# Keys, memories and values of a decoder step's cross-attention loaded through GpSimd's queue, one step earlier and by a clock of emitted work

## The chip, the cores and the metric

The kernel runs on one core of a Trainium2 chip. The metric is the device time of one execution in microseconds (us), as the median of several runs. TensorE is called PE in the profile (PEld is its weight load), VectorE DVE, ScalarE ACT, GpSimd POOL, SyncE SP.

## What is computed

One step of a one-layer decoder on 256 prompt tokens and 64 sample tokens (8 requests of 8 tokens) that share all weights, in float32. A mixer (retention heads beside a gated short convolution), a cross-attention over 256 memory tokens, and a SwiGLU feed-forward; each adds to the residual. The prompt's memory keys and values are products of this step; those of the eight sample requests come from a cache in HBM.

```python
def memory_kv(mem, ln_mem_g, w_mk, w_mv):
    B, N, _ = mem.shape
    hm = rmsnorm(mem, ln_mem_g)
    mk = (hm @ w_mk).reshape(B, N, XA_HEADS, XA_DIM)
    mv = (hm @ w_mv).reshape(B, N, XA_HEADS, XA_DIM)
    return mk, mv

def memory_xattn_sublayer(x, ln_g, w_xq, w_xo, mk, mv):
    B, T, _ = x.shape
    h = rmsnorm(x, ln_g)
    q = (h @ w_xq).reshape(B, T, XA_HEADS, XA_DIM).astype(jnp.float32)
    s = jnp.einsum('bthd,bnhd->bhtn', q, mk.astype(jnp.float32)) * (XA_DIM ** -0.5)
    p = jax.nn.softmax(s, axis=-1)
    o = jnp.einsum('bhtn,bnhd->bthd', p, mv.astype(jnp.float32)).reshape(B, T, D_MODEL)
    return x + o.astype(x.dtype) @ w_xo
```

Here XA_HEADS is 4, XA_DIM 512, D_MODEL 2048. The sample requests' keys and values are 16 MB each.

## The kernel before

Every product with a weight runs as three matmuls per tile (`mm3`, L163 to L165): activations and weights are split into a high and a low float32r part. `Weights` streams the weights: SP loads a chunk of 512 KB (`w_raw`, four buffers, three loaded ahead), ACT casts a piece of 128x512 to `w_hi` (L121), DVE subtracts for `w_lo` (L122). Five buffers of each part let ACT and DVE run three pieces ahead of PE. One piece is two k-rows of a product with 320 columns (twelve matmuls), or one k-row of `w_mk` or `w_mv` with 512 columns (six).

PE, ACT and DVE execute in the order in which the program text emits (`manual_schedule`), POOL and SP in theirs. Work beside the products is written as generators in a queue, `background`; after every piece `tick(rate)` lets the first generator go on by one `yield`.

The stages in order, in us of the profiled execution: retention and convolution products to 454.6; the product with `w_mix_out` (called the mixer's output product) to 567.3, in eight groups `g` of eight pieces, each followed by `residual` (L704); the product with `w_xq` in eight groups to about 700; per head of four, the products with `w_mk` and `w_mv`, to 941; the product with `w_xo` to 1066; the feed-forward to the end.

`residual` does for each of two rows `m`: DVE adds the product to `x_res` (L707), `split_gain` makes `a_hi` (ACT, L244) and `a_lo` (DVE, L245), and `add_square` (L292) lets ACT write the square to `sq_t` (L297), of which there is one buffer, and POOL add it to `sq_sum` (L298).

The cross-attention's side work:

- `fetch_memory` and `fetch_keys` load the prompt's memories and the samples' keys, 512 KB a tile, as four DMAs of 32 partitions each on SP's queue, into three buffers `keys`.
- `memory_tiles` turns a memory tile on DVE (L783), multiplies by the gain (L788), squares on ACT (L790) and splits into `mem_hi`, `mem_lo`, which lie in the mixer's buffers `b_hi`, `b_lo`. It begins with the product with `w_xq`.
- `sample_head(h)`, for each head and each half `p` of the requests: DVE turns four key tiles (L851) into four buffers `kt`, PE makes the scores (L860). Then `load_values` (L813) loads four tiles of 512 KB into the same four buffers on SP's queue, the exponents follow, and PE multiplies with the values (L887). The second half's values are loaded when the first's product has been emitted, with `PACE` (5) yields between.
- `prompt_scores`, `prompt_values` do the prompt's part of a head, from the fresh `mk` and `mv`. `kv` (one buffer) is written by ACT (L1006) and sent out on POOL's queue (L1007).

Of the kernel before, what the change touches and what calls it, by code (L numbers as in the profile page):

```python
# [11 lines left out]
F32 = mybir.dt.float32  # L12
# [24 lines left out]
RATE_RET, RATE_XQ, RATE_KV = 0.9, 1.0, 1.0  # L37
PACE = 5
# [97 lines left out]
def step_kernel(ctx, tc, a, o):  # L136
# [80 lines left out]
    def drain():  # L217
        while background:
            credit[0] = 1.0
            tick(0.0)  # L220

# [197 lines left out]
    def continue_product(acc, xh, xl, nk, rate, k_from, k_to, k_first=0):  # L419
        done = k_from  # L420
        while done < k_to:
# [7 lines left out]
            tick(rate)  # L429

# [8 lines left out]
    with tc.tile_pool(name="ret", bufs=2, reuse_waits="tile") as ret:  # L439
# [162 lines left out]
        for pair in range(4):  # L602
# [27 lines left out]
            if pair == 0:  # L630
# [5 lines left out]
                hold_b.tile([P, 120], F32, name="fill_b")  # L636
# [84 lines left out]
    for g in range(8):  # L721
        residual(g, product(b_hi, b_lo, KT, 0.25), LN_XA, a_hi, a_lo)
    background.append(norm_table(XD ** -0.5))


    with tc.tile_pool(name="att", bufs=1, reuse_waits="tile") as att:
        q_p = att.tile([P, KT, TP], F32, name="q_p")
# [5 lines left out]
        xq_done = []  # L733
# [6 lines left out]
        def kv_tile():  # L740
            return att.tile([P, 1024], F32, tag="kt", name=uid("kt"), bufs=4)

        def misc_tile():
            return att.tile([P, 512], F32, tag="misc", name=uid("misc"), bufs=2)

# [19 lines left out]

        mem_order = deque(range(4))

        def fetch_memory():


            i = mem_order.popleft()
            t = att.tile([P, 8, P], F32, tag="keys", name=uid("mem"), bufs=3)
            for d in range(4):
                DMA.dma_start(out=t[32 * d:32 * d + 32].rearrange("p (n m) d -> p n (m d)", n=2),
                              in_=a["mem_prompt"][0, 64 * i:64 * i + 64, XD * d:XD * d + XD]
                              .rearrange("(n q) d -> q n d", q=32))
            keys.append(t)

        def memory_tiles():
            for i in range(4):  # L780
                t = keys.popleft()
                kt = kv_tile().rearrange("p (n k q) -> p n k q", k=KT, q=32)
                V.transpose(out=kt, in_=t.rearrange("p (n m) d -> p n (m d)", n=2)  # L783
                            .rearrange("p n (c k) -> p n k c", k=KT))
                flat = t.rearrange("p (n m) d -> p n (m d)", n=2)
                for n in range(2):
                    if n:
                        V.tensor_tensor(out=kt, in0=kt, in1=g_mem.unsqueeze(1).unsqueeze(3)  # L788
                                        .to_broadcast([P, 2, KT, 32]), op=ALU.mult)
                    S.activation(out=misc_tile(), in_=flat[:, n, :], func=AF.Square,  # L790
                                 accum_out=ssq_mem[:, i // 2, 2 * (i % 2) + n:2 * (i % 2) + n + 1])
                    yield
                (fetch_keys if i else fetch_memory)()
                for n in range(2):
                    hi, lo = (m[:, :, 64 * i + 32 * n:64 * i + 32 * n + 32]
                              for m in (mem_hi, mem_lo))
                    split(hi, lo, kt[:, n])
                    yield
# [8 lines left out]
            yield  # L807
# [37 lines left out]
        def sample_head(h):  # L845
            ss = mix_tile()
            for p in range(2):
                kts = []
                for j in range(4):
                    kt = kv_tile().rearrange("p (n d c) -> p n d c", d=4, c=32)  # L850
                    V.transpose(out=kt, in_=keys.popleft().rearrange("p n (d c) -> p n d c", c=32))  # L851
                    fetch_keys()
                    kts.append(kt)
                    yield
                for _ in range(2):
                    yield
                for d in range(4):
                    for j in range(4):

                        PE.matmul(ss[32 * j:32 * j + 32, NM * p:NM * p + NM]  # L860
                                  .rearrange("q (n c) -> q n c", c=32),
                                  q_s[:, 4 * h + d, 16 * j:16 * j + 32], kts[j][:, :, d, :],
                                  start=(d == 0), stop=(d == 3), tile_position=(0, 32 * j),
                                  skip_group_check=True)
# [251 lines left out]
```

## Time and profile before

| what | value |
|---|---|
| median of 3 runs | 2017.84 us (2017.77 to 2021.89) |
| the profiled execution, its time | 2018.07 us |
| its span, first to last instruction | 2016.3 us |
| busy PE / DVE / ACT / POOL | 98% / 53% / 42% / 6% |
| granted clock of PE, mean | 0.997 |
| moved by SP's queue / POOL's queue | 329.72 MB / 9.05 MB |

Busy time of PE is the union of its matmuls, whose ends are modelled; a PE that waits in the midst of a group of small matmuls can show as busy. A timeline row gives the start, the length, the engine, the line, the operation and, in brackets, idle time of the engine ahead of it and what ended that. The granted clock 1.00 is 2.4 GHz, 0.50 is 1.2 GHz.

### The profile page before, as it was taken

How to read it: one execution, taken by the hardware profiler on the slowest of the kernel's cores; microseconds unless marked ns; L12 is line 12 of the kernel's file. 1: busy time of each engine (PE TensorE's matmuls, PEld its weight loads, DVE VectorE, ACT ScalarE, POOL GpSimd, SP SyncE). 2: the span in 40 equal slices, each digit the busy share in tenths (PEclk: the TensorE clock that was granted, in tenths of full speed). 3: DMA queues.
4: the chain of work that ended last, by engine and by line, in shares of the span. 5: the costliest groups of instructions: out<-in, count | busy, mean ns of one | idle time of the engine just before them, and what ended most of it. 6: DMA issues, size and time to landing. Idle time of an engine off the chain costs nothing.

```text
span 2016.3 us, 34017 instructions
## 1 busy us (share of the span) xinstructions
PE 1985.9 (98%) x13310; PEld 1907.1 (95%) x13310; DVE 1076.1 (53%) x1931; ACT 840.9 (42%) x1648; POOL 123.5 (6%) x230
## 2 busy tenths in 40 slices
PE   9999999999999999999999999999999999999997
PEld 8999999999998878778899999999999999999997
DVE  5556666555566545556454545544454544545433
ACT  6444433334454345444344434333343433334444
POOL 1111111110110000000010000000000000000010
PEclk9999999999999999999999999999999999999999
DMA  6465555445559965878545444444444444444443
GB/s 211 144 194 158 184 172 162 147 152 174 157 157 252 241 237 187 220 249 260 167 138 160 140 154 152 148 152 151 151 146 147 151 153 153 141 156 150 134 146 115
DMA packets 327664, 340.94 MB, mean 169 GB/s; under 512 B 13132, under 2 KB 296640, under 8 KB 327504
## 3 DMA queue, kind: packets, MB, share of 16 engines
q1 hardware_dynamic: 324240, 329.72, 53.1%
q0 software_dynamic: 3264, 9.05, 1.3%
q8 instruction: 104, 1.70, 0.4%
q14 instruction: 56, 0.46, 0.1%
HBM read 327.11 MB, written 11.61 MB: 168 GB/s over the span
## 4 chain that ended last, share of the span: by engine, by line
PE 92%; DMA 4%; DVE 2%; issue 1%; ACT 1%; SPq 0%; POOL 0%; POOLq 0%; DVEq 0%; ACTq 0%
PE acc L163 29%; PE acc L165 29%; PE acc L164 29%; DMA keys<-in_cache_mem_k_dram 2%; DMA kt<-in_cache_mem_v_dram 2%; PE mix L887 1%; PE mix L860 1%; DVE w_lo L122 1%; PE mix L375 0%; PE mix L165 0%; PE mix L163 0%; PE mix L164 0%; DVE kt L783 0%; DVE kt L851 0%; DMA x_tok<-in_x_prompt_dram 0%
## 5 line engine op out<-in xcount | busy, mean ns | idle before, releaser
L122 DVE TENSOR_TENSOR w_lo<-w_raw,w_hi 128x512 fp32r<-128x512 f32 x1072 | 711.6, 693 | 505.6 <-ACT w_hi L121 504.1
L121 ACT CAST w_hi<-w_raw 128x512 fp32r<-128x512 f32 x1072 | 631.2, 619 | 593.9 <-PE acc L164 520.9
L163 PE MATMUL acc<-a_hi,w_hi 128*128 128x320 f32 x2112 | 660.1, 313 | 3.4 <-ACT w_hi L121 3.1
L165 PE MATMUL acc<-a_hi,w_lo 128*128 128x320 f32 x2112 | 653.9, 310 | 0.7 <-DVE w_lo L122 0.7
L164 PE MATMUL acc<-a_lo,w_hi 128*128 128x320 f32 x2112 | 653.3, 309 | 0.0
L163 PE MATMUL acc<-b_hi,w_hi 128*128 128x320 f32 x1664 | 514.5, 309 | 0.0
L165 PE MATMUL acc<-b_hi,w_lo 128*128 128x320 f32 x1664 | 514.3, 309 | 0.0
L164 PE MATMUL acc<-b_lo,w_hi 128*128 128x320 f32 x1664 | 514.3, 309 | 0.0
L163 PEld LDWEIGHTS acc<-a_hi,w_hi 128*128 128x128 f32 x2112 | 397.1, 188 | 11.2 <-issue 5.3
L165 PEld LDWEIGHTS acc<-a_hi,w_lo 128*128 128x128 f32 x2112 | 397.2, 188 | 1.9 <-DVE w_lo L122 1.9
L164 PEld LDWEIGHTS acc<-a_lo,w_hi 128*128 128x128 f32 x2112 | 397.4, 188 | 0.8
L163 PEld LDWEIGHTS acc<-b_hi,w_hi 128*128 128x128 f32 x1664 | 312.4, 188 | 0.1
L164 PEld LDWEIGHTS acc<-b_lo,w_hi 128*128 128x128 f32 x1664 | 312.4, 188 | 0.0
L165 PEld LDWEIGHTS acc<-b_hi,w_lo 128*128 128x128 f32 x1664 | 312.4, 188 | 0.0
L298 POOL TENSOR_TENSOR sq_sum<-sq_sum,sq_t 128x320 f32<-128x320 f32 x43 | 38.3, 891 | 1125.7 <-ACT sq_t L297 1125.7
L164 PE MATMUL acc<-w_lo,b_hi 128*128 128x512 f32 x256 | 100.6, 393 | 3.3 <-DVE w_lo L122 3.3
L163 PE MATMUL acc<-w_hi,b_hi 128*128 128x512 f32 x256 | 102.5, 400 | 0.0
L165 PE MATMUL acc<-w_hi,b_lo 128*128 128x512 f32 x256 | 100.2, 391 | 0.0
L707 DVE TENSOR_TENSOR x_res<-x_res,acc 128x320 f32<-128x320 f32 x80 | 37.7, 486 | 74.9 <-PE acc L165 74.9
L163 PEld LDWEIGHTS acc<-w_hi,b_hi 128*128 128x128 f32 x256 | 48.4, 189 | 14.2 <-issue 5.0
L164 PEld LDWEIGHTS acc<-w_lo,b_hi 128*128 128x128 f32 x256 | 48.4, 189 | 13.4 <-DVE w_lo L122 4.4
L165 PEld LDWEIGHTS acc<-w_hi,b_lo 128*128 128x128 f32 x256 | 48.4, 189 | 10.4
(226 smaller groups left out, 1017.4 us busy)
## 6 DMA issues: line engine op xcount, KB each, us to landing
w_raw<-in_w_in_dram SPq DMA_DIRECT2D x112, 512.0 KB, 4.1
w_raw<-in_w_gate_dram SPq DMA_DIRECT2D x88, 512.0 KB, 4.1
w_raw<-in_w_up_dram SPq DMA_DIRECT2D x88, 512.0 KB, 4.3
w_raw<-in_w_down_dram SPq DMA_DIRECT2D x80, 512.0 KB, 3.3
w_raw<-in_w_mix_out_dram SPq DMA_DIRECT2D x32, 512.0 KB, 4.5
w_raw<-in_w_xq_dram SPq DMA_DIRECT2D x32, 512.0 KB, 5.0
keys<-in_cache_mem_k_dram SPq DMA_DIRECT2D x128, 128.0 KB, 5.2
kt<-in_cache_mem_v_dram SPq DMA_DIRECT2D x32, 512.0 KB, 7.5
```

What stands on the lines that cost most here:

```text
L121: self.nc.scalar.copy(out=hi, in_=src)
L122: self.nc.vector.tensor_tensor(out=lo, in0=src, in1=hi.bitcast(F32), op=ALU.subtract)
L163: PE.matmul(out, ah, bh, start=start, stop=False)
L164: PE.matmul(out, ah, bl, start=False, stop=False)
L165: PE.matmul(out, al, bh, start=False, stop=stop)
L298: G.tensor_tensor(out=sq, in0=sq, in1=t, op=ALU.add)
L707: V.tensor_tensor(out=x_res[:, m, :], in0=x_res[:, m, :], in1=ps[:, 0:T], op=ALU.add)
L860: PE.matmul(ss[32 * j:32 * j + 32, NM * p:NM * p + NM] .rearrange("q (n c) -> q n c", c=32), q_s[:, 4 * h + d, 16 * j:16 * j + 32], kts[j] ...
L887: PE.matmul(os[32 * j:32 * j + 32, :], pts[:, n, p, 32 * j:32 * j + 32], vs[j][:, n, :], start=(p == 0 and n == 0), stop=(p == 1 and n == ...
```

## The change

- Loads of keys, memories and values move from SP's queue to POOL's (`OUT`). A key tile becomes eight DMAs of 64 KB, a memory tile two of 256 KB, each to all 128 partitions; a value tile stays one DMA.
- The three `keys` and four `kt` buffers become nine shared buffers `slot`. Room comes from `q_p`, which loses head 0 (12 KB a partition for 16), and from the prompt's `pt`, which moves into `a_hi`, `a_lo`.
- The attention's pool is opened ahead of the mixer's output product. In that product, a generator `memories` fetches four memory tiles and four key tiles in its first step, turns and scales the memories, and fetches one more key tile for each. The splits into `mem_hi`, `mem_lo` stay behind that product, since `b_hi`, `b_lo` are its operands.
- Generators of the attention run as `flow`s: a `yield t` asks for `t` us on a clock that every emitted piece advances (0.88 us a k-row, 1.36 in `w_mk`, `w_mv`). All flows run side by side. A head of the samples starts 62 us of this clock behind the one before. Both halves' values have their own buffers; their products stand 24 us of the clock behind their loads and are emitted in two parts (`n`) with a step between.

```diff
-PACE = 5
+RATE_RET = 0.9
+US_ROW, US_KV = 0.88, 1.36
+HEAD_US, LOAD_US = 62.0, 24.0
...
+    def advance(us):
+        clock[0] += us
+        for f in list(flows):
+            while f[1] <= clock[0]:
+                step = next(f[0], None)
+                if step is None:
+                    flows.remove(f)
+                    break
+                f[1] = max(f[1], clock[0] - 0.5) + step
...
+            advance(kc * US_ROW)
...
-    for g in range(8):
-        residual(g, product(b_hi, b_lo, KT, 0.25), LN_XA, a_hi, a_lo)
-    background.append(norm_table(XD ** -0.5))
...
-        q_p = att.tile([P, KT, TP], F32, name="q_p")
+        q_p = att.tile([P, KT - 4, TP], F32, name="q_p")
         q_s = att.tile([P, KT, 80], F32, name="q_s")
         G.memset(q_s[:, :, 64:80], 0.0)
...
-        def kv_tile():
-            return att.tile([P, 1024], F32, tag="kt", name=uid("kt"), bufs=4)
+        def slot():
+            return att.tile([P, 1024], F32, tag="slot", name=uid("slot"), bufs=9)
...
-        def fetch_keys():
-            if not key_order:
-                return
-            h, b = key_order.popleft()
-            src = a["cache_mem_k"][0, b, :, h]
-            t = att.tile([P, 8, P], F32, tag="keys", name=uid("keys"), bufs=3)
-            for i in range(4):
-                DMA.dma_start(out=t[32 * i:32 * i + 32],
-                              in_=src[:, P * i:P * i + P].rearrange("(n q) d -> q n d", q=32))
-            keys.append(t)
...
+        def fetch_keys(n):
+            for _ in range(min(n, len(key_order))):
+                h, b = key_order.popleft()
+                t = slot().rearrange("p (m c) -> p m c", c=P)
+                src = a["cache_mem_k"][0, b, :, h]
+                for m in range(8):
+                    OUT.dma_start(out=t[:, m, :], in_=src[32 * m:32 * m + 32, :]
+                                  .rearrange("q (d c) -> d q c", d=4))
+                keys.append(t)
...
+        def fetch_memory(i):
...
+            t = slot().rearrange("p (n c) -> p n c", n=2)
+            for n in range(2):
+                at = 64 * i + 32 * n
+                OUT.dma_start(out=t[:, n, :], in_=a["mem_prompt"][0, at:at + 32, :]
+                              .rearrange("q (d c) -> d q c", d=4))
+            return t
...
+        def memories():
+            raw = [fetch_memory(i) for i in range(4)]
+            fetch_keys(4)
+            yield 14.0
+            turned = []
+            for i, t in enumerate(raw):
+                kt = q_room(i) if i < 3 else slot()
+                kt = kt.rearrange("p (n k q) -> p n k q", k=KT, q=32)
+                V.transpose(out=kt, in_=t.rearrange("p n (c k) -> p n k c", k=KT))
                 for n in range(2):
-                    if n:
...
-                    S.activation(out=misc_tile(), in_=flat[:, n, :], func=AF.Square,
+                    S.activation(out=misc_tile(), in_=t[:, n, :], func=AF.Square,
                                  accum_out=ssq_mem[:, i // 2, 2 * (i % 2) + n:2 * (i % 2) + n + 1])
...
+                fetch_keys(1)
+                yield 4.0
+                V.tensor_tensor(out=kt, in0=kt, in1=g_mem.unsqueeze(1).unsqueeze(3)
+                                .to_broadcast([P, 2, KT, 32]), op=ALU.mult)
+                turned.append(kt)
+                yield 4.0
...
+            while not xq_begun:
+                yield 1.0
+            yield 6.0
+            for i in (3, 0, 1, 2):
+                for n in range(2):
+                    hi, lo = (m[:, :, 64 * i + 32 * n:64 * i + 32 * n + 32]
+                              for m in (mem_hi, mem_lo))
+                    split(hi, lo, turned[i][:, n])
+                    yield 2.0
+            flow(samples())
...
-                t = kv_tile().rearrange("p (n d) -> p n d", d=XD)
-                DMA.dma_start(out=t, in_=a["cache_mem_v"][0, 2 * j + p, :, h]
+                t = slot().rearrange("p (n d) -> p n d", d=XD)
+                OUT.dma_start(out=t, in_=a["cache_mem_v"][0, 2 * j + p, :, h]
                               .rearrange("(n p) d -> p n d", p=P))
...
+        def until(t):
+            return max(0.5, t - clock[0])
+        def samples():
+            for h in range(XH):
+                kts = yield from turn_keys()
+                while heads_ready[0] <= h:
+                    yield 1.0
+                began = clock[0]
+                ss = mix_tile()
+                sample_scores(h, ss, 0, kts)
+                vs = [load_values(h, 0)]
+                yield 2.0
+                kts = yield from turn_keys()
+                sample_scores(h, ss, 1, kts)
+                second = clock[0]
+                vs.append(load_values(h, 1))
+                yield 1.0
+                e, rc = exponents(ss, "s")
+                V.tensor_tensor(out=rc, in0=rc, in1=own[:, 0:2], op=ALU.mult)
+                V.tensor_scalar(out=e[:, 0, :], in0=e[:, 0, :], scalar1=rc[:, 0:1], scalar2=None,
+                                op0=ALU.mult)
+                V.scalar_tensor_tensor(out=e[:, 0, :], in0=e[:, 1, :], scalar=rc[:, 1:2],
+                                       in1=e[:, 0, :], op0=ALU.mult, op1=ALU.add)
...
+                yield 6.0
+                ps = mix_tile()
+                    PE.transpose(ps[:, P * n:P * n + P], e[:, 0, P * n:P * n + P], ident)
+                for p in range(2):
+                    for n in range(2):
+                        V.tensor_copy(out=part(pts[:, n, p, :], 32, p),
+                                      in_=part(ps[:, P * n:P * n + P], 32, p))
+                os = None
+                for p, since in enumerate((began, second)):
+                    yield until(since + LOAD_US)
+                    os = os or mix_tile()
+                    for n in range(2):
+                        for j in range(4):
+                            PE.matmul(os[32 * j:32 * j + 32, :], pts[:, n, p, 32 * j:32 * j + 32],
+                                      vs[p][j][:, n, :], start=(p == 0 and n == 0),
+                                      stop=(p == 1 and n == 1), tile_position=(0, 32 * j),
+                                      skip_group_check=True)
+                        yield 1.0
+                    fetch_keys(4)
+                osb = misc_tile()
+                S.copy(out=osb, in_=os)
+                yield 2.0
+                if xq_done:
+                    sample_outputs(h, osb)
+                else:
+                    waiting.append((h, osb))
+                yield until(began + HEAD_US - 10.0)
...
+            pt = [t[:, 4 * h + 2:4 * h + 4, 0:TP] for t in (a_hi, a_lo)]
...
+        q_hi, q_lo = (t.rearrange("p (d t) -> p d t", t=TP) for t in (rest_hi, rest_lo))
+        flow(memories())
         for g in range(8):
-            for i, ps in enumerate(product(a_hi, a_lo, KT, RATE_XQ if g else 1.0)):
+            residual(g, product(b_hi, b_lo, KT, 0.25), LN_XA, a_hi, a_lo)
+        background.append(norm_table(XD ** -0.5))
+        xq_begun.append(True)
+        for g in range(8):
+                q = q_p[:, k - 4, :] if k >= 4 else misc_tile()[:, 0:TP]
+                V.tensor_tensor(out=q, in0=ps[:, 0:TP], in1=r_tab[:, 0:TP], op=ALU.mult)
+                if k < 4:
+                    split(q_hi[:, k, :], q_lo[:, k, :], q)
...
+                    heads_ready[0] += 1
...
-                    tick(RATE_KV)
+                    advance(US_KV)
...
-        drain()
+        run_out()
```

Of the functions not shown: `sample_scores`, `exponents` and `sample_outputs` issue what they issued before.

## Rows read from the trace of the kernel before

**Rows 1.** Windows: us, busy (count) per engine, PE first; clock, DMA share, GB/s.
```profile
454.00:567.00 113.00, 113.00 (x773) 113.00 (x772) 59.30 (x96) 50.30 (x94) 11.64 (x13) 1.00 0.53 165
...
620.00:725.00 105.00, 98.61 (x678) 79.50 (x677) 53.84 (x92) 37.05 (x98) 3.46 (x12) 1.00 0.98 271
...
840.00:856.00 16.00, 12.73 (x52) 9.98 (x51) 8.46 (x11) 6.29 (x11) 0.72 (x1) 0.89 1.13 252
```

**Rows 2.** Waits of PE, 573 to 988: us in total, times, longest.
```profile
PE mix L887 <- DMA kt<-in_cache_mem_v_dram: 6.0, 11, 1.7
PE acc L164 <- DVE w_lo L122: 3.3, 2, 2.6
PE acc L163 <- ACT w_hi L121: 3.1, 3, 1.3
```

**Rows 3.** Timeline of PE: two groups of products with values.
```profile
651.85 1.02 PE L887 MATMUL mix<-kt,pts 128*32 128x512 f32 x2 [1.75 <-DMA kt<-in_cache_mem_v_dram]
...
657.62 0.41 PE L163 MATMUL acc<-a_hi,w_hi 128*128 128x320 f32 x1
...
666.61 1.99 PE L887 MATMUL mix<-kt,pts 128*32 128x512 f32 x16
668.53 0.41 PE L163 MATMUL acc<-a_hi,w_hi 128*128 128x320 f32 x1
```

**Rows 4.** Timeline of PE: a group of scores, and a wait for weights.
```profile
693.66 0.63 PE L860 MATMUL mix<-kt,q_s 128*32 128x256 f32 x6
...
697.38 0.41 PE L163 MATMUL acc<-a_hi,w_hi 128*128 128x320 f32 x1 [0.78 <-ACT w_hi L121]
...
845.32 0.39 PE L163 MATMUL acc<-w_hi,b_hi 128*128 128x512 f32 x1
848.26 0.50 PE L164 MATMUL acc<-w_lo,b_hi 128*128 128x512 f32 x1 [2.55 <-DVE w_lo L122]
```

**Rows 5.** Windows again: the stretch behind that wait.
```profile
850.00:853.00 3.00, 3.00 (x11) 2.61 (x10) 2.85 (x5) 1.69 (x3) 0.00 (x0) 0.50 1.11 314
```

**Rows 6.** DMA issues: count, KB each, median us to landing.
```profile
kt<-in_cache_mem_v_dram SPq DMA_DIRECT2D x32, 512.0 KB, 7.5
```

**Rows 7.** Groups of DVE, 573 to 988: busy us, mean ns, idle before.
```profile
L851 DVE STREAM_TRANSPOSE kt<-keys 128x1024 f32<-128x1024 f32 x32 | 39.6, 1239 | 17.8 <-DMA keys<-in_cache_mem_k_dram 13.9 <-PE mix L860 2.3 <-PE acc L165 1.5
...
L783 DVE STREAM_TRANSPOSE kt<-mem 128x1024 f32<-128x1024 f32 x4 | 8.0, 1997 | 0.0
```

**Rows 8.** Timeline of POOL and DVE where the mixer's output product begins.
```profile
451.33 0.54 POOL L748 MEMSET pts<- 128x512 f32 x1
...
454.39 0.49 DVE L699 TENSOR_TENSOR mixed<-acc,cv 128x320 f32<-128x320 f32 x1 [1.88 <-PE acc L165]
```

**Rows 9.** Groups of POOL: its DMA issues, 64 KB and 512 KB.
```profile
L523 POOL DMA_DIRECT2D out_ret_p_dram<-sp x8 | 5.0, 622 | 19.0 <-ACT sp L522 19.0
...
L1007 POOL DMA_DIRECT2D out_mk_dram<-kv x4 | 3.0, 750 | 108.7 <-ACT kv L1006 108.7
```

**Rows 10.** Timeline of POOL: two DMA issues in a row.
```profile
331.74 0.53 POOL L655 DMA_DIRECT2D out_conv_p_dram<-tail  x1 [2.59 <-ACT tail L653]
332.26 0.52 POOL L656 DMA_DIRECT2D out_conv_s_dram<-tail  x1
```

**Rows 11.** Timelines of DVE, ACT and POOL: the residual step of g=1.
```profile
482.55 0.49 DVE L707 TENSOR_TENSOR x_res<-x_res,acc 128x320 f32<-128x320 f32 x1 [1.88 <-PE acc L165]
...
485.12 0.45 ACT L297 ACTIVATE sq_t<-x_res 128x320 f32<-128x320 f32 x1
485.48 2.17 ACT L121 CAST w_hi<-w_raw 128x512 fp32r<-128x512 f32 x4
...
485.65 0.89 POOL L298 TENSOR_TENSOR sq_sum<-sq_sum,sq_t 128x320 f32<-128x320 f32 x1 [0.69 <-ACT sq_t L297]
...
486.12 3.38 DVE L122 TENSOR_TENSOR w_lo<-w_raw,w_hi 128x512 fp32r<-128x512 f32 x5 [0.32 <-ACT w_hi L121]
```

**Rows 12.** Tile sq_t: who waited for its addition on POOL, us, times.
```profile
  ACT sq_t L297: 5.9, 6
```

More of the change, by code (lines that the diff above doesn't have):

```diff
@@ L220, in drain, with flow, run_out @@
             tick(0.0)
+    flows, clock = [], [0.0]
+    def flow(steps):
+        flows.append([steps, clock[0]])
+    def advance(us):
[7 more added lines that the diff above has]
+                f[1] = max(f[1], clock[0] - 0.5) + step
+    def run_out():
+        while flows:
+            advance(1.0)
     ident = const.tile([P, P], F32, name="ident")
@@ L768, in fetch_memory @@
[L768 to L785, printed above, removed]
+        def fetch_keys(n):
[7 more added lines that the diff above has]
+                keys.append(t)
@@ new lines, in turn_keys, with sample_scores @@
+        def turn_keys():
+            kts = []
+            for _ in range(4):
+                kt = slot().rearrange("p (n d c) -> p n d c", d=4, c=32)
+                V.transpose(out=kt, in_=keys.popleft().rearrange("p n (d c) -> p n d c", c=32))
+                kts.append(kt)
+                yield 2.4
+            return kts
+        def sample_scores(h, ss, p, kts):
+            for d in range(4):
+                for j in range(4):
+                    PE.matmul(ss[32 * j:32 * j + 32, NM * p:NM * p + NM]
+                              .rearrange("q (n c) -> q n c", c=32),
+                              q_s[:, 4 * h + d, 16 * j:16 * j + 32], kts[j][:, :, d, :],
+                              start=(d == 0), stop=(d == 3), tile_position=(0, 32 * j),
+                              skip_group_check=True)
@@ L912, in sample_outputs @@
                       real16(ps[:, P * d:P * d + P]))
-            yield
         prompt_pt = {}
         def prompt_scores(h, kp):
-            yield
-            q_hi, q_lo = (t.rearrange("p (d t) -> p d t", t=TP) for t in (rest_hi, rest_lo))
-            split(q_hi, q_lo, q_p[:, 4 * h:4 * h + 4, :])
+            yield 1.0
+            if h:
+                split(q_hi, q_lo, q_p[:, 4 * h - 4:4 * h, :])
             k_hi, k_lo = (t[:, 4 * h:4 * h + 4, 0:NM] for t in (a_hi, a_lo))
@@ L926, in prompt_scores @@
                       ps.rearrange("p (d n) -> p d n", n=NM))
-            for _ in range(3):
-                yield
+            yield 4.0
             ps = mix_tile()
@@ L938, in prompt_scores @@
                                 scalar2=None, op0=ALU.mult)
-            for _ in range(3):
-                yield
+            yield 4.0
             ps = mix_tile()
@@ L945, in prompt_scores @@
                                  e[:, t, P * n:P * n + P], ident)
-            pt = [att.tile([P, 2, TP], F32R, tag=f"pt{i}", name=uid("pt")) for i in range(2)]
+            pt = [t[:, 4 * h + 2:4 * h + 4, 0:TP] for t in (a_hi, a_lo)]
             split(pt[0], pt[1], ps.rearrange("p (n t) -> p n t", t=TP))
             prompt_pt[h] = pt
-            yield
+            yield 1.0
         def prompt_values(h, vp):
@@ L954, in prompt_values @@
             split(v_hi, v_lo, vp)
-            for _ in range(3):
-                yield
+            yield 4.0
             for dd in range(2):
```

91 lines of the change are left out of this document (9 added, 82 removed).

## The prediction

> **What bounds the kernel now.** I read the windows first [rows 1]. PE sets the end: in the mixer's output product it is busy in 113.00 of 113.00 us, and the other engines and the DMAs (share 0.53) have room. Only the attention, 573 to 988, has holes: from 620 to 725 PE is busy in 98.61 of 105 us while the 16 DMA engines stand at 0.98, and from 840 to 856 in 12.73 of 16. The list of PE's waits says for what [rows 2]: 6.0 us for values, 3.3 for `w_lo`, 3.1 for `w_hi`. That is less than is lost, since a group of small matmuls that waits between its members shows as busy. So I measured groups in PE's timeline from their first matmul to the next product's first.
>
> Values: a group of 16 matmuls takes 666.61 to 668.53, 1.9 us, when its tiles are there, and 651.85 to 657.62, 5.8 us, when they land one by one [rows 3]. Four of eight groups are of the long kind (the first and the last, at 651.85 and at 967.09, within 0.1 us of each other): 4 x 3.85 = 15.4 us. The first had to wait 1.75 us before it could begin [rows 3], the second 0.6, and one of the short ones is 0.3 longer than the rest: together 18.1 us. Scores: a group takes 1.87 us, but 693.66 to 697.38 is 3.72 [rows 4]; with three smaller ones, 3.2 us. Weights: 845.32 to 848.26 is 2.7 us over the usual step [rows 4]; with the one before it, those near 602, 635 and 697 and the slow restart after each, 7.9 us. Behind the 2.7 us the granted clock reads 0.50, 1.2 GHz, for 3.4 us [rows 5], which costs 1.7. Around the last head's end, 1.0. **Sum of what can be won: 31.9 us.** PE's own work stays, so no time under 2018.07 - 31.9 = 1986.2 is in reach.
>
> **The change, part by part.** The sum is made against the profiled execution, 2018.07 us (span 2016.3), 0.23 over the median.
>
> *Loads leave SP's queue.* Keys and values no longer stand between weight loads, and weights not behind a wait for a free buffer. A value tile lands 7.5 us after its issue when four crowd in [rows 6]; its product now stands 24 us of emitted work behind its load, and keys are fetched at least 25 us ahead. The 18.1 and 3.2 us should go. Cover: the DMA share of 0.98 holds from 620 to 725 [rows 1]; the new start of one head in 62 us spreads the 32 MB over some 290 us. Without that cover the value waits come back whole, 18 us.
>
> *Weights.* The waits at 842 to 848 came from DVE's transposes that waited for keys (13.9 us of such idle time in all [rows 7]); they go with their clock loss, 4.9 + 1.7 us of the above. Those at 602, 635 and 697 come at the end of a `w_xq` group, where DVE and ACT carry `q_p`, `q_s` and side work at once. The memories' transposes (4 x 2.0 us [rows 7]) and scalings leave that stage, but splits and key transposes stay in it. I leave 1.5 of some 3 us standing, bounds 0 and 4.
>
> *Value products in two parts.* Eight groups more to enter and leave. Entering and leaving a group is an estimated 0.3 us (behind one, the first matmul of a product lasts 0.41 us for 0.31 [rows 3], and the small ones must run out), so 8 x 0.3 = 2.4 us are lost, bounds 0.8 and 4.
>
> *The memories' stage in the mixer's output product.* DVE gets 4 x 2.0 us and 4 x 1.2 us, ACT eight squares, over some 40 us; DVE is busy 59.30 of 113 there [rows 1] and three pieces ahead of PE. I cost them at nothing; without that lead, at their length, 13 us.
>
> *POOL's queue in that product.* This is the new wait. The first step issues 8 + 32 DMAs, the next two steps 8 each, at 15.8 and 24.6 us of the product; both stand on POOL ahead of the additions of `residual` for g=1 (28.2), the first step ahead of that for g=0. When POOL can begin: `q_p` is 4 KB smaller, so `q_s` begins 12288 bytes above the pools' base, over the convolution's last tiles (`cv`, 9472 to 15616 by the sizes in the code). Its memset, done by 451.3 before, now waits for DVE's reading of them, until 454.88 [rows 8]; with both memsets (0.54 the larger) POOL is free at 455.8. An issue of 64 KB to 128 rows costs 0.62 us [rows 9], two in a row follow each other at their length [rows 10]; the 512 KB with twice the rows cost 0.75. All 56 DMAs here have 128 rows: I take 0.62 each. Bounds: 0.52, a row of two to eighteen rows [rows 10], and 0.75.
>
> With i for that price, the addition for m=2 ends at 455.8 + 56 i + 2 x 0.89 = 457.6 + 56 i, two additions of 0.89 [rows 11] among it. There is one `sq_t`: ACT's square of m=3, at 485.12 before, must wait for that, and the next `w_hi` stands behind it on ACT, the `w_lo` behind that on DVE [rows 11]. That ACT waits so for POOL is in the trace already, six times [rows 12]. How late may it be? The cast starts 0.36 and the subtraction 1.00 us behind the square's start, and ends 0.69 later. PE ends the group at 482.4 and has three pieces of 1.76 us, until 487.7, needing `w_lo` 0.3 later: the square must start by 486.3. So PE stands still for 457.6 + 56 i - 486.3 = 56 i - 28.7 us: 6.0 at 0.62, 0.4 at 0.52, 13.3 at 0.75. A 2.7 us stand brought the half clock; I add the same 1.7 us.
>
> Later POOL has time: a head's 64 key DMAs and eight values take 64 x 0.62 + 8 x 0.75 = 46 us of at least 62. `kv`'s write-out can stand up to 20 us behind key DMAs; with 6 us to land it just ends before the next `kv`, 28 us on. Nothing, bounds 0 and 3.
>
> *Sum:* -31.9 + 1.5 + 2.4 + 6.0 + 1.7 = -20.3, or **1998 us**.
>
> The Trainium skill has a rule against this change ("SBUF: two separate sides" in "SBUF — State Buffer"): a DMA issued from GpSimd needs its descriptors written by GpSimd, which is shut out while DVE runs in a two-port mode; it gives 620 ns alone and about 3100 overlapped. The eight issues of 64 KB here lie beside a busy DVE and took 0.62 on average [rows 9], so these do not show it; by the rule's 3100 the formula would give 145 us, an estimate from that page.
>
> **The rivals.**
>
> *A. POOL is out of the way.* If the memset does not wait, or the price is nearer 0.5, the stand falls to 0 to 2 us and no half clock follows: 1998 - 6.0 - 1.7 = 1990, down to 1986 if the 2.4 and 1.5 vanish too. For: the overlap is read from sizes, not from rows. Against: the price of 128 rows is eight times the same.
>
> *B. POOL's issue is dearer in a long row.* No row shows more than two in a row. At 0.75 the stand is 13.3, so 2005; at 0.90, 21.7, so 2014. **Slower:** the 20.3 won are gone when 56 i - 28.7 reaches 26.3, i = 0.98, and from i = 1.06 the kernel is slower by over 0.2%, at 1.1 us 2025. For: 512 KB issues cost 0.75. Against: those have more rows. The skill's lock would be such a price.
>
> *C. The values are late all the same.* If the DMA engines are the limit and not the order on SP, the 18.1 us stay: 2016. For: share 0.98 over 105 us. Against: the mean there is 271 GB/s while the head's loads bunch, and the stages on both sides stand near 0.6.
>
> **How the numbers follow.** Forecast (1994 to 2002) 0.50; A 0.27; B without a loss 0.10, B slower 0.05; C 0.08. The predicted time is the forecast's. The range takes A's floor and B up to 0.83 us an issue: 1986 to 2010. A measurement here tells 0.2%, 4 us, from no change. Faster by more: 0.50 + 0.27 + most of B and none of C, 0.87; the same 0.07; slower 0.06.
>
> **What would show it.** In the new profile: the products with values in groups of about 1.2 us with no DMA wait; no wait for keys at DVE's transposes; in the mixer's output product one stand of PE of some 6 us near 488, ended by `w_lo` or `w_hi`, with ACT's `sq_t` waiting for POOL and POOL's key issues back to back at 0.62, and a few us of half clock behind it. If PE runs through that product, A holds; if values still land into their group, C.

## The result, and the profile after

| | before | after |
|---|---|---|
| median, runs side by side | 2018.66 us (2017.77 to 2021.89) | 2032.86 us (2030.47 to 2034.98) |
| the profiled execution's span | 2016.3 us | 2033.2 us |
| granted clock of PE, mean | 0.997 | 0.989 |

The ratio is 1.0067 (95% interval 1.0050 to 1.0085): the kernel became slower by 14 us, where 20 less were forecast. The time lies outside the range of 1986 to 2010, and the sign was wrong.

Where the time came from is seen when the span is cut where PE's products begin. The windows of the kernel before, with the columns of [rows 1], are the mixer's output product, the product with `w_xq`, the products of the memories (`w_mk`, `w_mv`) and the product with `w_xo`:

```profile
454.60:567.30 112.70, 112.70 (x771) 112.70 (x770) 59.36 (x97) 50.30 (x94) 11.64 (x13) 1.00 0.53 164
567.30:713.40 146.10, 138.21 (x970) 121.28 (x969) 89.67 (x144) 64.44 (x168) 8.78 (x20) 1.00 0.83 230
713.40:940.90 227.50, 222.49 (x1176) 176.96 (x1176) 130.05 (x208) 106.76 (x204) 5.18 (x7) 0.99 0.75 222
940.90:1066.00 125.10, 122.88 (x832) 117.13 (x831) 62.93 (x107) 53.80 (x103) 12.36 (x14) 1.00 0.54 174
```

And the same four of the changed kernel:

```profile
454.60:599.30 144.70, 116.45 (x779) 114.54 (x778) 71.29 (x107) 55.03 (x110) 62.01 (x88) 0.91 0.63 161
599.30:725.50 126.20, 125.92 (x916) 118.15 (x915) 74.01 (x125) 59.66 (x144) 54.77 (x86) 1.00 0.76 198
725.50:967.20 241.70, 233.73 (x1262) 177.75 (x1261) 137.40 (x231) 109.28 (x222) 111.44 (x165) 0.99 0.90 243
967.20:1083.10 115.90, 115.75 (x794) 115.49 (x793) 60.09 (x96) 52.29 (x97) 12.27 (x14) 1.00 0.48 154
```

The mixer's product went from 112.7 to 144.7 us (+32.0). The other three stages together went from 498.7 to 483.8 (-14.9): -19.9, +14.2 and -9.2. Behind them nothing moved.

The waits of PE from 454 to 1083 (us in total, times, longest), to hold against [rows 2]:

```profile
PE acc L167 <- ACT w_hi L125: 28.5, 3, 25.1
PE mix L854 <- ACT kv L1049: 5.5, 3, 5.0
PE acc L168 <- DVE w_lo L126: 1.1, 2, 0.9
PE acc L169 <- DVE w_lo L126: 1.0, 3, 0.5
```

The waits for values are gone. A group of products with values is now eight matmuls and takes 1 us; [rows 3] has the long and the short group of before:

```profile
675.64 1.06 PE L934 MATMUL mix<-slot,pts 128*32 128x512 f32 x8
676.63 0.41 PE L167 MATMUL acc<-a_hi,w_hi 128*128 128x320 f32 x1
```

In their place there are two new stands (stretches in which PE stands still): one of 25 us that ACT's `w_hi` ends, one of 5 us that ACT's `kv` ends.

**The stand of 25 us.** ACT's timeline in the mixer's product, to hold against [rows 11]:

```profile
487.88 0.56 ACT L268 ACTIVATE a_hi<-x_res,gains 128x320 fp32r<-128x320 f32 x1 [3.11 <-DVE x_res L732]
501.75 0.47 ACT L321 ACTIVATE sq_t<-x_res 128x320 f32<-128x320 f32 x1 [13.31 <-POOL sq_sum L322]
502.13 0.55 ACT L268 ACTIVATE a_hi<-x_res,gains 128x320 fp32r<-128x320 f32 x1
513.29 0.47 ACT L321 ACTIVATE sq_t<-x_res 128x320 f32<-128x320 f32 x1 [10.61 <-POOL sq_sum L322]
```

The square of m=3 starts at 513.29, not at 485.12, since the addition of m=2 on POOL comes so late; the cast of the next weights stands behind it, and PE stands from 489.3 to 514.3. What POOL does meanwhile:

```profile
455.64 1.44 POOL L797 DMA_DIRECT2D slot<-in_mem_prompt_dram  x2
457.59 4.03 POOL L797 DMA_DIRECT2D slot<-in_mem_prompt_dram  x6 [0.51 <-DVE b_lo L274]
461.61 0.68 POOL L787 DMA_DIRECT2D slot<-in_cache_mem_k_dram  x1
464.35 0.68 POOL L787 DMA_DIRECT2D slot<-in_cache_mem_k_dram  x1 [2.07 <-DMA slot<-in_mem_prompt_dram]
467.28 0.68 POOL L787 DMA_DIRECT2D slot<-in_cache_mem_k_dram  x1 [2.25 <-DMA slot<-in_mem_prompt_dram]
...
494.83 6.01 POOL L787 DMA_DIRECT2D slot<-in_cache_mem_k_dram  x9 [2.72 <-DMA slot<-in_cache_mem_k_dram]
500.85 0.87 POOL L322 TENSOR_TENSOR sq_sum<-sq_sum,sq_t 128x320 f32<-128x320 f32 x1
501.65 10.71 POOL L787 DMA_DIRECT2D slot<-in_cache_mem_k_dram  x16
512.38 0.87 POOL L322 TENSOR_TENSOR sq_sum<-sq_sum,sq_t 128x320 f32<-128x320 f32 x1
```

POOL begins at 455.64, as forecast (455.8), and issues 40 loads, an addition, 16 loads and the next addition, as forecast. An issue takes 0.68 us. But the first row is not back to back: from the tenth load on POOL stands between issues until an earlier load has landed, although every `slot` written here is used for the first time. The semaphores in the trace say which: POOL's loads use eight of them in turn, and the second key load, at 464.35, goes 0.28 us after the load eight places ahead (issued 456.38) landed at 464.07. The third goes 0.28 behind the landing at 467.00, and so on wherever POOL stands in this row (only the fourth, at 470.69, goes 1.37 behind, and the trace doesn't tell why). No more than eight loads are under way on this queue at a time. Each issue itself waits for its semaphore, so this limit is one that the compiled program contains; no run had more semaphores, and how many loads the hardware alone would let be under way is not shown. The Trainium skill says where such a wait is spent ("DMA: Bandwidth & Descriptors", "Anatomy of one DMA — SWDGE (gpsimd) path"): on the issuing engine's sequencer, before dispatch. The trace agrees: the addition in the queue stood through it.

The price of the stand is also the clock. Windows of the same stretch (clock third from the end):

```profile
485.00:495.00 10.00, 4.25 (x30) 3.99 (x28) 3.79 (x7) 0.56 (x1) 5.55 (x9) 0.82 0.96 171
495.00:505.00 10.00, 0.00 (x0) 0.00 (x0) 0.55 (x1) 0.92 (x2) 9.98 (x15) 0.50 0.30 81
505.00:515.00 10.00, 0.68 (x2) 0.50 (x2) 0.70 (x1) 1.71 (x4) 9.97 (x16) 0.50 0.35 95
515.00:525.00 10.00, 9.92 (x57) 9.70 (x57) 9.95 (x11) 5.67 (x14) 4.95 (x7) 0.82 0.85 204
```

The granted clock falls to 0.50 (1.2 GHz) while PE stands and stays there for its first 4 us of work, which costs some 2 us. A second stand of 2.2 us, at 530.8, has the same chain: the next addition, at 531.07, stands behind eight further key loads.

**The stand of 5 us.** Timelines of ACT, POOL and PE in the second product of the memories:

```profile
818.06 1.26 ACT L1049 ACTIVATE kv<-acc,r_mem 128x512 f32<-128x512 f32 x2 [9.03 <-DMA out_mv_dram<-kv]
...
810.97 0.76 POOL L1050 DMA_DIRECT2D out_mv_dram<-kv  x1 [1.20 <-DMA slot<-in_cache_mem_k_dram]
...
818.80 0.34 PE L854 MATMUL mix<-ident,kv 128*128 128x128 f32 x1 [4.97 <-ACT kv L1049]
```

There is one `kv` buffer. It was full at 784.9. Its write-out was issued at 810.97, since 56 key loads stand ahead of it on POOL behind the write-out before (758.2). It landed at 818.0, and only then could ACT write the next `kv`, for which PE waited since 813.8. At 877 and 908 ACT waits so again, 2.1 and 5.7 us, and PE stands for up to 1.3.

### The profile page after: what moved, and what is told of

The parts are those of the page before. It is cut to its first block, busy times and chain, and to the rows that moved or that the text cites. A ratio compares the mean times of both kernels' runs of the same rounds, so it can differ in the third digit from the quotient of the medians.

```text
span 2033.2 us, 34239 instructions
## 1 busy us (share of the span) xinstructions
PE 1981.4 (97%) x13310; PEld 1904.9 (94%) x13310; DVE 1077.3 (53%) x1934; ACT 842.1 (41%) x1651; POOL 326.0 (16%) x526
## 4 chain that ended last, share of the span: by engine, by line
PE 65%; DMA 5%; issue 1%; POOL 1%; DVE 1%; ACT 1%; POOLq 0%; DVEq 0%; ACTq 0%
PE acc L167 21%; PE acc L169 21%; PE acc L168 21%; DMA slot<-in_cache_mem_k_dram 4%; POOL slot L787 1%; DMA w_raw<-in_w_mv_dram 1%; PE mix L890 1%; PE mix L934 0%; DMA w_raw<-in_w_mk_dram 0%; DMA out_mk_dram<-kv 0%; DMA out_mv_dram<-kv 0%; DVE w_lo L126 0%; PE mix L167 0%; PE mix L168 0%; PE mix L169 0%
## 5 line engine op out<-in xcount | busy, mean ns | idle before, releaser
L787 POOL DMA_DIRECT2D slot<-in_cache_mem_k_dram x256 | 172.4, 679 | 78.0 <-DMA slot<-in_cache_mem_k_dram 29.1
```

The costliest lines, as they stand in the source:

```text
L787: OUT.dma_start(out=t[:, m, :], in_=src[32 * m:32 * m + 32, :] .rearrange("q (d c) -> d q c", d=4))
```

## The experiments

The theory is that the losses are two waits behind POOL's row of loads, that of the additions of squares (32 us) and that of the write-out of `kv` (some 7), and that the row is long because of waits for landings. The rivals: the loads crowd the weights out of the DMA engines, and POOL's order only hides it; the price lies in the number of issues, or in their pieces; the queue itself is the gain or the loss. Medians of before lay between 2019.57 and 2019.90 in these comparisons.

**The additions on DVE.** Edit:

```
-            G.tensor_tensor(out=sq, in0=sq, in1=t, op=ALU.add)
+            add.tensor_tensor(out=sq, in0=sq, in1=t, op=ALU.add)
...
-                add_square(sq_sum, x_res[:, m, :], m == 0)
+                add_square(sq_sum, x_res[:, m, :], m == 0, V if base == LN_XA else G)
```

> The changed kernel with one edit: in the mixer's output product the additions of squares into sq_sum run on DVE and not on POOL, so they no longer stand behind the loads that POOL issues. Theory (ACT's next square waits for an addition queued on POOL behind 40 to 56 loads): the stand of 25.2 us at 489, the smaller ones at 530 and 533 (2.9) and the half clock behind them (1.9) go, the row of loads on POOL stays as long as it is: 2033 - 30 = 2003 us, between 1998 and 2010; the stand of 5.1 us for kv in the product of the memories stays. Rival (the loads crowd the weights of w_mix_out out of the DMA engines, and POOL's order only hides it): PE stands still for w_raw instead, 10 us or more of it, and the time is 2013 or above.

Measured: 2004.24 us, ratio 0.9921 (0.9898 to 0.9943). POOL's row is as long as it was, but nothing in that product stands behind it any more; the waits of PE for `w_hi` are down to

```profile
PE acc L167 <- ACT w_hi L125: 2.4, 2, 2.1
```

and the mixer's product takes 119.1 us. The theory holds, the rival falls as the main cause. It has a remainder: 119.1 is 6.4 above before, and ACT now waits 20.1 us in that product for weights to land, of which before shows none.

**kv from ACT's queue.** Edit:

```
-                OUT.dma_start(out=dst[0, 0, :, h].rearrange("(j p) d -> p j d", p=P), in_=kv)
+                S.dma_start(out=dst[0, 0, :, h].rearrange("(j p) d -> p j d", p=P), in_=kv)
```

> The changed kernel with one edit: kv is written out from ACT's DMA queue, directly behind the activations that fill it, and not from POOL's behind the key loads. Theory (there is one kv buffer; its write-out is issued late on POOL, and the next activation into kv waits for it to land): the stand of 5.1 us at 813 and the 1.7 us of half clock behind it go, 2033 - 7 = 2026 us, 2023 to 2029. Rival (the write-out is late since the DMA engines are full at that place, share 0.97, and lands late whoever issues it): no more than 2 us are won, 2031 to 2033.

Measured: 2025.12 us, ratio 1.0029 (1.0018 to 1.0040). The three stages behind the mixer's product:

```profile
599.80:726.00 126.20, 125.92 (x915) 118.15 (x915) 73.91 (x125) 59.65 (x144) 55.26 (x86) 1.00 0.74 199
726.00:955.00 229.00, 228.87 (x1261) 175.89 (x1260) 137.25 (x231) 110.51 (x222) 105.63 (x157) 1.00 0.93 255
955.00:1070.90 115.90, 115.75 (x793) 115.46 (x792) 60.07 (x96) 52.39 (x97) 11.58 (x13) 1.00 0.48 155
```

The products of the memories take 229.0 us instead of 241.7, at a DMA share of 0.93, so the engines were not too full for it: the rival falls. In the traces the edit wins 12.7 us, by the medians 7.7: the changed kernel's profiled execution is the slowest of its four, this run's the fastest of its ten.

**The loads on SP's queue.** `OUT.dma_start` becomes `DMA.dma_start` in `fetch_keys`, `fetch_memory` and `load_values`.

> The changed kernel with the loads of memories, keys and values issued on SP's queue again, among the weights, and all else as it is (slots, clocked samples, 8 loads to a key tile). If the gain in the attention comes from the queue: the waits for values and weights come back, some 18 us, while the stand in the mixer's product (30 with its clock) and the one for kv (7) go, so about 2014 us. If it comes from the clocked order and the early fetches: those stay away and it is about 1996 us. A third way: the key loads, each with its wait for a free slot or for an earlier landing, hold SP's weight loads already in the mixer's product, and ACT's casts wait for w_raw there: above 2020 us.

Measured: 2126.47 us, ratio 1.0523 (1.0506 to 1.0540): the third way, and far above its bound of 2020. SP's timeline where the mixer's product begins:

```profile
455.46 9.75 SPq L797 DMA_DIRECT2D slot<-in_mem_prompt_dram  x7
465.26 35.22 SPq L787 DMA_DIRECT2D slot<-in_cache_mem_k_dram  x32
500.58 3.66 SPq L113 DMA_DIRECT2D w_raw<-in_w_mix_out_dram  x4
```

The same rows of loads now hold the weights: PE stands 32.8 us here and 8.7 to 18.3 us at six later places. So moving the loads off SP is needed with this order and this number of loads, and the row, not POOL as such, is what blocks.

**A key tile in four loads.** `for m in range(8)` over `t[:, m, :]` becomes four loads of `t[32 * d:32 * d + 32]`, as before had them.

> The changed kernel with a key tile loaded in four DMAs of 128 KB (32 rows of partitions each, as the kernel before has them) and not eight of 64 KB. In the first steps POOL then issues 32 loads ahead of the additions of the second pair and not 56. If POOL's row is slow because of the number of issues, 0.68 us each and a wait with it: 32 x 0.94 = 30 us, the stand falls from 25.2 to about 1 to 2 us and the time to some 2005 us. If an issue costs POOL by the pieces of 512 bytes that it must describe (256 to a load and not 128): the row is as long as before or near it, and the stand 15 to 25 us, 2020 to 2033 us. If it waits for landings of the load eight places ahead (wait of one load for an earlier one), each of twice the bytes: in between, 32 x 1.25 = 40 us of row, a stand of some 11 us, about 2017 us.

Measured: 2010.93 us, ratio 0.9944 (0.9923 to 0.9965), between the first case (2005) and the third (2017). An issue takes 0.58 us, less than one of half the bytes. The first addition of the row comes at 490.1, after 24 loads that need 8 x 0.68 + 16 x 0.58 = 14.7 us and take 35.0: most of the row is waiting for landings here too. These loads took 11.6 us on average to land, an eighth of that is 1.45 us, and the row takes 35.0 / 24 = 1.46 a load. ACT's squares wait for POOL only 3.1 us in all, yet the mixer's product takes 134.2 us, with stands of up to 4.6 us for `w_hi`. That these aren't POOL's was shown by a later run. More than half of what this run wins lies elsewhere: the products of the memories take 228.6 us and not 241.7, as with `kv` from ACT's queue, since the write-out of `kv` now goes at most 5.3 us after `kv` is full, and not 26.1.

**Both edits together**, additions on DVE and `kv` from ACT's queue:

> The changed kernel with both edits of the two runs before: the additions of squares in the mixer's product on DVE, and kv written out from ACT's queue. If the two losses are independent they add up: the first edit alone gave 2004.2, the second won 7.7, so 1996.5 us, 1993 to 2000. If they overlap (with PE standing less in the mixer's product the later loads bunch against the weights of w_mk and w_mv in another way), 2000 to 2004. By the prediction's own sum without its POOL and kv terms, 2018.1 - 31.9 + 1.5 + 2.4 = 1990 us; what is left above that is the crowding of w_mix_out's weights by the memories and keys, some 6 us.

Measured: 1997.60 us, ratio 0.9891 (0.9872 to 0.9910). The losses add up. The mixer's product takes 116.9, the rest of the attention 471.3 us.

**Both edits and a key tile in four loads:**

> The changed kernel with the additions on DVE, kv from ACT's queue and a key tile in four loads of 128 KB, not spread. POOL has 128 issues fewer, but the same bytes move at the same places. If only the crowding of the DMA engines is left, this is within 2 us of the run with eight loads to a tile (1996.5 expected); if POOL's time still matters somewhere in the attention, where loads stand behind each other, up to 4 us less.

Measured: 2010.26 us, ratio 0.9951 (0.9934 to 0.9967): 13 us slower than with eight loads, outside what was expected. No square waits for POOL in this kernel, and its mixer's product takes 133.3 us, as with four loads alone. So those stands are weights: ACT waits 22.7 us for `w_raw` of `w_mix_out` there, against 11.6 with eight loads to a tile, and the slowest of these weights take 22.2 us to land, against 16.5. The sum of ACT's waits alone doesn't set the time, though: the run with the additions on DVE has 20.1 us of them in a product of 119.1, the last of the spread runs below 26.2 in one of 118.7. Why loads of 128 KB to 32 partitions delay the weights more than loads of 64 KB to 128 stays open. With eight under way they also have twice the bytes under way, and no run separates that from the partitions.

**The loads spread by the clock.** Edit:

```
-            raw = [fetch_memory(i) for i in range(4)]
-            fetch_keys(4)
-            yield 14.0
+            raw = []
+            for i in range(4):
+                raw.append(fetch_memory(i))
+                yield 6.0
...
-                yield 4.0
+                yield 7.0
+                fetch_keys(1)
...
-                yield 4.0
+                yield 7.0
```

> The changed kernel with the loads in the mixer's product spread by the clock: two memory loads every 6 us, then one key tile (8 loads) every 7 us, in place of 40 loads at once and 8 every 4 us; the additions stay on POOL, kv too. Theory (the row of loads on POOL, lengthened by the limit of eight in flight, holds the additions): no row is longer than 8 x 0.68 = 5.4 us, an addition is at most that late, against a slack of 1.2 us, so at each of the four or five pairs beside key loads PE stands 0 to 4 us, 8 in all: 2033 - 31 + 8 = 2010 us, 2003 to 2020. Rival (the sum of the loads counts, not their order: POOL and the DMA engines are short of time over the whole product): the stand stays above 15 us, 2020 or more.

Measured: 2020.67 us, ratio 1.0003 (0.9987 to 1.0018). The stand is still 17.7 us, as the rival had it, but the trace shows another reason:

```profile
480.50 5.54 POOL L787 DMA_DIRECT2D slot<-in_cache_mem_k_dram  x8 [2.12 <-DMA slot<-in_mem_prompt_dram]
486.06 0.89 POOL L322 TENSOR_TENSOR sq_sum<-sq_sum,sq_t 128x320 f32<-128x320 f32 x1
...
497.96 8.02 POOL L787 DMA_DIRECT2D slot<-in_cache_mem_k_dram  x12 [0.24 <-issue]
506.00 0.87 POOL L322 TENSOR_TENSOR sq_sum<-sq_sum,sq_t 128x320 f32<-128x320 f32 x1
```

Ahead of the first addition stand all eight memory loads and 15 key loads, 24 more ahead of the next, though the program emits most of them later. `manual_schedule` keeps the emitted order on PE, ACT and DVE alone; a planner places POOL's instructions, and it had pulled the loads forward. The loads weren't spread. Two runs with `ENG.Pool` added to `manual_schedule` tell the two apart; the first is the changed kernel with only that:

> The changed kernel with POOL's instructions in the order in which the program emits them (POOL was not among the engines whose order the program keeps, so a planner had placed them; with the loads spread by the clock it had moved 24 loads ahead of an addition that the program emits before most of them). Here the first row stays 40 loads and then 16, only the two additions of the second pair stand together. Control for the run beside it: the stand in the mixer's product stays at 25 us or more and the time at 2033, within 4 us. If the planner's order of POOL had been part of the loss, below 2025.

> The loads spread by the clock as in the run before, and POOL's instructions in the order of emission, so that the additions really stand between the loads: 4 memory loads ahead of the first addition, then 4, then 16 key loads between pairs of additions that come every 14 us. Theory (only the length of the row between two additions counts): 16 loads take 16 x 0.68 = 10.9 us and, if they wait little for landings, fit between the pairs; no stand of PE ended by POOL longer than 2 us; the mixer's product falls from 144.7 to some 117 us; the stand for kv stays; 2033 - 28 = 2005 us, 1999 to 2010. Rival (loads wait so long for the load eight before them that 16 of them take over 14 us beside the weights): stands of some us at each of four pairs, 2012 or more.

Measured: 2034.59 us (1.0065; 1.0049 to 1.0082) with the order alone, its stand 23.5 us where 25 or more were expected, and 2006.30 us (0.9925; 0.9910 to 0.9940) with the order and the spreading. So the planner's order of POOL explains next to nothing of the changed kernel's loss, and the row's length between two additions makes 26 of the 32 us that the mixer's product lost. With the order and the spreading POOL does

```profile
504.25 6.03 POOL L787 DMA_DIRECT2D slot<-in_cache_mem_k_dram  x9
...
516.04 0.68 POOL L787 DMA_DIRECT2D slot<-in_cache_mem_k_dram  x1 [0.42 <-DMA slot<-in_cache_mem_k_dram]
516.73 0.89 POOL L322 TENSOR_TENSOR sq_sum<-sq_sum,sq_t 128x320 f32<-128x320 f32 x1
```

16 loads in 12.5 us between additions, PE has no stand over 0.5 us in the mixer's product, and that takes 118.7 us. The stand for `kv` stays, 5.8 us. With `kv` from ACT's queue besides:

> As the run beside it, with kv written out from ACT's queue besides. Nothing is moved off POOL in the mixer's product. If rows and the kv write-out are all that the change lost, the attention takes what the sum without them gives: 1990 us plus what the loads take from w_mix_out's weights, 2 to 6 us: 1992 to 1997. If the additions on POOL cost something beside 16 loads: 1998 to 2004.

Measured: 1998.01 us, ratio 0.9881 (0.9863 to 0.9899), 1 us above the range of the first case and at the lower end of the second, in which the additions on POOL cost something beside 16 loads. The two can't be told apart by this time. And with the additions on DVE, where nothing in POOL's queue paces the loads:

> The changed kernel with the additions on DVE, kv from ACT's queue and the loads in the mixer's product spread as in the run beside it (two memory loads every 6 us, then a key tile every 7 us). If what is left in that product, some 6 us, is w_mix_out's weights that land late beside a burst of 4 MB, spreading it takes most of this away: 1991 us, 1988 to 1994. If the weights are late for another reason (the transposes and splits on DVE and ACT between them): as without the spreading, 1996 or 1997.

Measured: 1996.96 us, ratio 0.9885 (0.9869 to 0.9902): as without the spreading. With nothing between them on POOL the loads go out as fast as earlier ones land (DMA share 1.17 from 470 to 485, and 1.16 without the spreading), so this run says little on a spread. The run before it, where the additions do pace the loads, has 119.7 us for the product, no less. Three versions between 1997 and 1998 us beat both kernels and can't be told from one another.

**The memories' stage behind the mixer's product.** `flow(memories())` moves behind the loop over `residual`.

> The changed kernel with the memories' stage begun behind the mixer's output product and not in it, everything else as changed: that part alone is undone. If that early stage is what cost the 32 us of the mixer's product, the product is back at 113 us. What else it brings: the samples begin some 45 us of emitted work later, so the last head's products fall behind the products of the memories, into the first product with w_xo, where little is left beside them; there PE stands for keys or values. If that costs nothing: 2033 - 32 = 2001 us. If it costs the remainder of a head's loads, 10 to 20 us: 2011 to 2021, which I hold likelier.

In this kernel the turned memories and the prompt's queries share `q_p`'s room at the same time and overwrite each other, so `mk`, `mv` and `y_p` hold other values; the work is the same. Measured: 2036.59 us, ratio 1.0074 (1.0053 to 1.0096). It did not undo the part: the mixer's product still takes 134.8 us with a stand of 18.0, since the planner again pulled the loads forward on POOL (the first memory load is issued at 455.9). What the early stage alone buys isn't told by this run.

## Why the prediction was wrong, point by point

- **What bounds the kernel, and the 31.9 us to be won:** right as to what PE waited for; that the sum came out within 0.4 us is in part luck. Take `kv`'s wait away, and the stages from `w_xq` to `w_xo` take 471.1 us against 498.7: 27.6 less, where -31.9 + 2.4 + 1.5 = -28.0 was forecast. Values and keys go as said. Of the weights' waits near 602 to 697 next to nothing stays, where 1.5 us were left standing: PE is busy in 125.92 of the 126.20 us of `w_xq`. With that and the next point the sum would have been -29.7, and where the other 2 us went no run tells. The waits that [rows 7] show for keys are down from 13.9 to 2.5 us. Rival C falls.
- **Value products in two parts:** no stand at their entries, and the size nearly right. From the product's last matmul ahead of a group to its first one behind, less the usual step of 0.15 us, a group of 16 that didn't wait took 1.94 us before (at 958.0) and one of eight 1.09 now (at 675.64). Each split costs 0.24 us, eight of them 1.9 where 2.4 were forecast.
- **The wait for POOL, its place and its chain:** right. The memset waits (3.84 us in the trace, for DVE), POOL begins at 455.64, one stand near 489 ended by `w_hi`, `sq_t` waiting for POOL, half clock behind it. So rival A falls.
- **Its size: the step that failed.** The formula 457.6 + 56 i took an issue to be all that a load costs POOL. The addition ends at 513.25 instead of 492.3. Of the 21 us, 56 issues at 0.68 instead of 0.62 make 3.4, and the gaps in the first row, added up, make 18.1: 0.5 of a wait for DVE and 17.6 of waits for the load eight places ahead. The stand was 25.1 us and not 6.0. With its echo at 530, the half clock and some 3 us besides, the product lost 32.0 where 7.7 were forecast. The effective price, (513.25 - 457.6) / 56 = 0.99 us, is over rival B's break-even of 0.98. B had the right place and sign, at a chance of 0.15, of which 0.05 for slower, but its mechanism, a dearer issue, is the smaller part: an issue cost 0.06 more, the waits between issues the rest. By its formula 0.99 gives 2019, and `kv` makes up most of what is left. Against the profiled execution, 2034.98 and 37 us over the forecast, the account is 24.3 in the product, 12.7 for `kv` and 0.4 by which less was won.
- **This could have been read before.** I looked for long rows on POOL, where there were none, and took the issue's length from rows of two [rows 10]. SP's queue had rows of key loads, and its waits in the trace of before (us, times, longest) and its loads' times to landing show the limit:

```profile
SPq L762 <- DMA keys<-in_cache_mem_k_dram: 12.3, 36, 2.3
...
DMA to landing us min/median/max: 2.3/5.2/9.7
```

  None of the 128 key loads there goes ahead of the landing of SP's load eight places before it, and where SP waits the load follows within some 0.1 us (691.07 behind 691.06, 691.89 behind 691.83). The loads took a median of 5.2 and up to 9.7 us to land. An eighth of that is 0.65 to 1.2 us a load: the bounds for i should have been these, and slower would not have had 0.06. The changed kernel agrees: in its first row a load takes 7.8 us on average to land, an eighth is 0.98, and the row takes 1.13 a load; in the row of 16, with PE and the weights standing still, it lands in 3.0, an eighth is 0.37, and the row takes its issues, 0.67 each.
- **kv's write-out: sized at nothing, 0 to 3.** It was delayed by 26.1 us and not 20, and landed in 7.0 and not 6 (before, the write-outs took 3.7 to 8.4), so it needed 33 us where there were 28. This cost 12.7 us in the trace of the products of the memories (the stands, their half clock, the later ones). The cause is the same: between two write-outs on POOL stand up to 56 key loads, and these wait for landings too.
- **The memories' work on DVE and ACT, at nothing:** not the main loss, but not nothing. In all versions without long stands the mixer's product takes 116.9 to 119.7 us against 112.7. What that is differs from run to run. In the run with both edits PE's longest stand, 1.9 us, is ended by `w_hi`, and ACT waits 11.6 us for weights, a term that the prediction did not have: a load of `w_mix_out` lands after a median of 7.6 us there, against 4.6 before. With the loads spread and POOL's order kept, ACT waits for no weights at all, and yet the product takes 118.7 us. There PE waits for DVE (us, times, longest):

```profile
PE acc L169 <- DVE w_lo L126: 3.2, 8, 0.5
```

  Four of these eight waits end some 0.6 us behind a memory's transpose of 2.0 us on DVE, which the prediction had costed at nothing because DVE is three pieces ahead of PE. How the rest divides stays open.
- **The lock of GpSimd by DVE** (the Trainium skill, "SBUF — State Buffer", "SBUF: two separate sides"): its 3100 ns do not show. 256 key loads beside a busy DVE took 675 to 828 ns, median 677. Whether DVE ran in a two-port mode beside them, which is the rule's condition, the trace doesn't tell.

## What to carry to other kernels

Price a row of loads on a queue by the issue's length and by landing time over the number of loads that may be under way (eight here), whichever is longer; the waits of another queue in the same trace can show that number. Then ask what else stands in that queue behind the row, and who waits for it: here an addition of 0.9 us and one write-out turned 28 us of gain into 14 us of loss. Put the row where nothing short stands behind it, or the short work on another engine. When you spread loads, make sure that the engine's order is the one you wrote: here the spreading won 12 us without POOL's order kept and 27 with it.

## What was not expected of the hardware

- A load of 64 KB to 128 partitions took POOL 0.68 us to issue, one of 128 KB to 32 partitions 0.58: twice the pieces of 512 bytes, and a shorter issue.
- Key tiles in four loads of 128 KB to 32 partitions delayed the weights beside them more than in eight of 64 KB to 128: the same bytes in all, 133.3 against 116.9 us for the product. Whether it is the partitions or the bytes under way is not shown.
- On SP a key load of 64 KB to 128 partitions took a median of 0.76 us to issue and up to 4.5, against 0.68 and up to 0.83 on POOL.
